# A hybrid SSD, GLA and ConvFFN decoder step: alternating accumulator banks, half a gate projected early, weighted scan steps, a late memory norm and ordered state loads

## The chip, the core and the metric

The kernel runs on one core of a Trainium2 chip. The metric is device microseconds of one execution, lower is better. A core has five engines that run their own instruction streams: TensorE (PE in the profile, with its weight loads as PEld), VectorE (DVE), ScalarE (ACT), GpSimd (POOL) and SyncE (SP). [...] Matmul results land in PSUM, which has eight banks of 512 fp32 words per partition.

## What is computed

One inference step of one layer, for 256 prompt tokens and 8 x 4 sample tokens with the same weights (288 columns in all). All data is fp32.

```python
xn = rmsnorm(x, norm_mix)
z, xbc, dt, q, k, v, r, g_lr, gate_a, gate_b = split(xn @ w_in)
# branch a: causal conv, silu, SSD scan (4 groups of 8 heads), D skip, silu(z), group norm
branch_a = u @ w_ssd_out
# branch b: gated linear attention, 4 heads of 256 keys x 512 values, head norm, silu(r)
branch_b = o @ w_gla_out
merged = sigmoid(gate_a) * branch_a + sigmoid(gate_b) * branch_b
h = x + merged @ w_mix_out
h = h + cross_attend(rmsnorm(h, norm_cross), mem_k, mem_v, w_cq, w_co)   # 256 memory tokens
h = h + conv_ffn(rmsnorm(h, norm_ffn))                                     # w_up, conv of 3, silu gate, w_down
y = rmsnorm(h, norm_final)
```

For the prompt, `mem_k` and `mem_v` are `rmsnorm(mem_prompt, norm_mem) @ w_ck` and `@ w_cv`, and they are outputs too. For the samples they come from a cache. The scans start from zero for the prompt and from `state_ssd` and `state_gla` for the eight samples; the new states are outputs.

## The kernel before

Activations lie transposed: 16 tiles (KT) of 128 features by 288 tokens. Weights stream from HBM, 512 KB at a time, on SP's queue (`wload`, L102 to L105, three buffers `raw`). Each weight tile is split into two parts in a reduced fp32 format: ACT writes `whi` (L97), DVE the remainder `wlo` (L99), five buffers each. `proj_w` (L114) then makes three matmuls of 128 x 128 weights by 288 tokens for each k tile and output tile: high by high (L129), high by low (L130), low by high (L133). Up to two output tiles of a projection are accumulated at a time, in banks from `acc_tile` (L56), one tag with four buffers. Three more banks serve everything else (`mm_tile`), one the long sums of the scans (`la_tile`).

The order of work is written as generators. `proj` (L140) yields once per two k tiles. `weave` (L154) takes the main generator step by step and in between so many steps of a background generator that `n_bg` of them are spread over `n_main` main steps. A scheduler then fixes each engine's order from this program order and its own priorities; `keep_in_program_order` and `high_priority` are hints to it.

- Memory part: `mem_proj` (L287) makes the keys or values of one head, 512 columns, with matmuls L313, L314 and L317. The first runs under a hand-fixed order and prepares its operands on the way (`prep_mem`, L324). At its last k tile it computes the memory norm: a reduction, Ln (L336) and Exp (L337) on ACT; each head is scaled by it when it leaves PSUM. `x_norm` (L370) and `x_prep` (L406) normalise x and build masks (L429, L432) in the background of the next heads.
- Eight units: SSD groups 0 to 3, then GLA heads 0 to 3. In stage n (the loop at L1149) the scan of unit n is the background; the main work is 12 steps of the projections of unit n + 1, the output projection of unit n - 1 (`out_proj`, L890, with the additions L897), and the rest of unit n + 1. `N_MAIN` and `N_BG` are the weave's two counts of each stage. In stage 7 the main work is gate A (`gate_a`, L1111).
- SSD scan (L650): POOL loads decays (`load_decay`, L658), and the sample states in four pairs (`load_state`, L672). States are transposed on TensorE and copied by ACT to `st` (L824), which L807 reads; L834 updates the states, and SP stores them.
- GLA scan (L969): POOL loads eight states of 512 KB (L976), four first, then one more after each of the first four is updated. L1078 multiplies queries by the states of half q = 0 or 1; it reads state 3 or 7 first. L1086 and L1087 update a state, L1090 stores it on SP. States and prompt sums share the buffers of `c4`.
- Gate A: ma, the SSD branch, goes to DRAM (`ma_d`) after stage 4's output projection; `gate_a` reads two tiles at a time, multiplies and stores to `mg_d`. Gate B (L1177) adds both branches. Then come mix_out, cross-attention, and the FFN, whose convolution columns are loaded and transposed (L1425) at its beginning.

Of the kernel before, what the change touches and what calls it, by code (L numbers as in the profile page):

```python
# [8 lines left out]
F32 = mybir.dt.float32  # L9
# [26 lines left out]
N_MAIN = [32, 64, 48, 64, 64, 64, 64, 80]  # L36
N_BG = [48] * 4 + [38] * 4
# [3 lines left out]
def hybrid_step(ctx: ExitStack, tc: tile.TileContext, I: dict, O: list):  # L41
# [14 lines left out]
    def acc_tile():  # L56
        return ps.tile([P, 512], F32, tag="acc", bufs=4, name="acc")
# [140 lines left out]
    def rstd_from(pl, ssq, n, four=False):  # L198
# [13 lines left out]
    bsel = p1.tile([NS, NB, NL], F32, name="bsel")  # L212
    G.affine_select(bsel, ones[0:NS, 0:NS], pattern=[[-4, NB], [0, NL]], compare_op=ALU.is_ge, fill=0.0, base=0,
                    channel_multiplier=1)
    G.affine_select(bsel, bsel, pattern=[[4, NB], [0, NL]], compare_op=ALU.is_ge, fill=0.0, base=3, channel_multiplier=-1)
# [12 lines left out]
    dtbd = p1.tile([P, 32 + 40], F32, name="dtbd")[:, 0:32]  # L228
# [16 lines left out]
    mg_d = dram.tile([P, KT, T], F32, name="mg_d")  # L245
    x_d = dram.tile([P, KT, T], F32, name="x_d")
# [3 lines left out]
    with pool("p0") as p0:  # L250
# [3 lines left out]
        bsel_rep = p0.tile([NS, 4, NS], F32, name="bsel_rep")  # L254
        V.tensor_copy(bsel_rep, bsel.rearrange("p b l -> p (b l)").unsqueeze(1).to_broadcast([NS, 4, NS]))
        bsel_rep = bsel_rep.rearrange("p r t -> p (r t)")
        smask = p0.tile([NS, NS], F32, name="smask")
        G.affine_select(smask, causal[0:NS, 0:NS], pattern=[[-4, NB], [0, NL]], compare_op=ALU.is_ge, fill=0.0, base=0,
                        channel_multiplier=1)
        irep = p0.tile([NS, 4, NS], F32, name="irep")  # L260
        V.tensor_copy(irep, ident[0:NS, 0:NS].unsqueeze(1).to_broadcast([NS, 4, NS]))
# [5 lines left out]
        mrow = p0.tile([KT, P], F32, name="mrow")  # L267
        S.dma_start(out=mrow, in_=I["norm_mem"].rearrange("(t p) -> t p", p=P))
# [8 lines left out]
        def mem_prep(k):  # L277

            a = acc_tile() if k % 2 else mm_tile()
# [3 lines left out]

        mss = p0.tile([P, 2, 4], F32, name="mss")
        mrs = p0.tile([P, 2], F32, name="mrs")

        def mem_proj(w, hd, dst, prep=None):  # L287
# [15 lines left out]
            accs = [acc_tile() for _ in range(2)]  # L303
# [15 lines left out]
            t = p0.tile([P, 2, 512], F32, tag="mp", bufs=2, name="mp")  # L319
            for m in range(2):  # L320
                S.activation(t[:, m, :], accs[m], ACT.Identity, scale=mrs[:, m:m + 1])
            G.dma_start(out=dst[0, :, hd, :].rearrange("(m p) d -> p m d", p=P), in_=t)

        def prep_mem(kk):  # L324
            if kk == 0:
                a = mm_tile()
                TR(a[:, 0:KT], mrow, ident[0:KT, 0:KT])
                V.tensor_copy(gmem, a[:, 0:KT])
# [5 lines left out]
            if kk == KT - 1:  # L334
                V.tensor_reduce(mrs, mss, AX.X, ALU.add)
                S.activation(mrs, mrs, ACT.Ln, scale=1.0 / D, bias=epsc[:, 0:1])  # L336
                S.activation(mrs, mrs, ACT.Exp, scale=-0.5)  # L337

        with tc.manual_schedule(engines={mybir.EngineType.PE, mybir.EngineType.Activation, mybir.EngineType.DVE,
# [4 lines left out]
            run(mem_proj(I["w_ck"], 0, o_pmk, prep_mem))  # L344
# [61 lines left out]
        def x_prep():  # L406
# [21 lines left out]
            a = mm_tile()  # L428
# [682 lines left out]
    def gate_a(t, a):  # L1111
# [9 lines left out]
        if t % 2:  # L1121
            nc.sync.dma_start(out=mg_d[:, t - 1:t + 1, :], in_=m)
# [502 lines left out]
```

## Time and profile before

| What | Value |
|---|---|
| Median of 3 runs | 2608.87 us (2606.83 to 2610.24) |
| The profiled execution's own time | 2607.92 us |
| Its span | 2606.2 us |
| Mean granted TensorE clock | 0.996 |
| Read from and written to HBM | 465.27 MB and 45.48 MB |

In the profile, busy times overlap between engines, and a matmul's length includes its way through the array, so that the distance between two starts, not the length, is what a matmul takes from TensorE. A row of the timeline reads: start, length, engine, line, operation, output and operands, shapes, and how many instructions of one kind follow each other in that row; in brackets stands the idle time of the engine before it and what ended it. Rows of windows give the busy time of each engine and number of instructions in a stretch, the granted clock as a share of full speed, the share of the DMA engines, and GB/s. "DMA to landing" is the time from the issue of a transfer to its completion.

### The profile page before, as it was taken

The numbers are of one execution on the slowest core, as the hardware profiler recorded it, in microseconds if no ns is written. First come the engines' busy times: TensorE is split into PE (matmuls) and PEld (weight loads), VectorE is DVE, ScalarE is ACT, GpSimd is POOL, SyncE is SP. The second block draws the span as 40 slices with busy tenths as digits, with TensorE's granted clock in tenths as the row PEclk, the third lists the DMA queues.
The fourth block names the chain that finished last, engine by engine and source line by source line (L and its number), as shares of the span: only waits on it lengthen the run. The fifth ranks groups of instructions, "written<-read, shape, count | busy, mean of one in ns | idle before, by whom it ended". The sixth has DMA issues, their size and how long they took to land. (4 is left out here: it accounts for less than half of the span.)

```text
span 2606.2 us, 50491 instructions
## 1 busy us (share of the span) xinstructions
PE 2576.2 (99%) x19123; PEld 2473.3 (95%) x19123; DVE 1718.2 (66%) x3683; ACT 1376.2 (53%) x2796; POOL 308.2 (12%) x425
## 2 busy tenths in 40 slices
PE   8999999999999999999999999999999999999998
PEld 7889999999989998999999989899999999999998
DVE  5655786886766566666666555567777677675765
ACT  7655655564645463534455544455545454454545
POOL 2003021100000000000000222202202020110200
PEclk9999999999999999999999999999999999999999
DMA  7666566665676666777666778655555555555553
GB/s 250 208 225 205 179 200 179 201 195 148 201 234 212 199 213 218 225 233 237 182 207 214 246 262 298 213 166 168 166 170 166 168 161 172 168 160 178 164 171 126
DMA packets 435280, 514.07 MB, mean 197 GB/s; under 512 B 23208, under 2 KB 384984, under 8 KB 434716
## 3 DMA queue, kind: packets, MB, share of 16 engines
q1 hardware_dynamic: 408684, 423.16, 52.5%
q0 software_dynamic: 26320, 87.68, 10.1%
q8 instruction: 150, 2.46, 0.4%
q14 instruction: 94, 0.77, 0.1%
q10 hardware_dynamic: 32, 0.01, 0.0%
HBM read 465.27 MB, written 45.48 MB: 196 GB/s over the span
## 5 line engine op out<-in xcount | busy, mean ns | idle before, releaser
L99 DVE TENSOR_TENSOR wlo<-raw,whi 128x512 fp32r<-128x512 f32 (+1 forms) x1464 | 989.5, 689 | 703.3 <-ACT whi L97 689.6
L97 ACT CAST whi<-raw 128x512 fp32r<-128x512 f32 (+1 forms) x1464 | 898.2, 618 | 1043.8 <-PE acc L130 824.1
L129 PE MATMUL acc<-xn,whi 128*128 128x288 f32 (+1 forms) x1936 | 551.0, 300 | 2.8 <-ACT whi L97 2.8
L130 PE MATMUL acc<-xn,whi 128*128 128x288 f32 (+1 forms) x1936 | 542.5, 295 | 0.0
L133 PE MATMUL acc<-xn,wlo 128*128 128x288 f32 (+1 forms) x1936 | 413.0, 295 | 1.4 <-DVE wlo L99 1.4
L129 PE MATMUL acc<-hf,whi 128*128 128x288 f32 x1408 | 396.0, 296 | 0.0
L130 PE MATMUL acc<-hf,whi 128*128 128x288 f32 x1408 | 393.5, 295 | 0.0
L129 PEld LDWEIGHTS acc<-xn,whi 128*128 128x128 f32 (+1 forms) x1936 | 365.0, 189 | 10.2 <-issue 6.7
L130 PEld LDWEIGHTS acc<-xn,whi 128*128 128x128 f32 (+1 forms) x1936 | 365.2, 189 | 4.2 <-issue 1.0
L133 PEld LDWEIGHTS acc<-xn,wlo 128*128 128x128 f32 (+1 forms) x1936 | 311.3, 188 | 1.8 <-DVE wlo L99 1.7
L133 PE MATMUL acc<-hf,wlo 128*128 128x288 f32 x1408 | 302.2, 296 | 0.0
L130 PEld LDWEIGHTS acc<-hf,whi 128*128 128x128 f32 x1408 | 265.1, 188 | 0.1
L129 PEld LDWEIGHTS acc<-hf,whi 128*128 128x128 f32 x1408 | 264.7, 188 | 0.1
L133 PEld LDWEIGHTS acc<-hf,wlo 128*128 128x128 f32 x1408 | 225.4, 188 | 0.0
L130 PE MATMUL acc<-pr,whi 128*128 128x288 f32 x704 | 196.6, 295 | 0.0
L129 PE MATMUL acc<-pr,whi 128*128 128x288 f32 x704 | 195.9, 294 | 0.0
L129 PE MATMUL acc<-un,whi 128*128 128x288 f32 x512 | 153.3, 315 | 2.3 <-DVE mb L897 1.0
L133 PE MATMUL acc<-pr,wlo 128*128 128x288 f32 x704 | 147.8, 291 | 0.0
L1457 POOL COPY fsp<-fst 128x16 f32<-128x16 f32 x88 | 105.4, 1222 | 335.3 <-ACT fcg L1463 87.8
L130 PE MATMUL acc<-un,whi 128*128 128x288 f32 x512 | 143.2, 295 | 0.0
L130 PEld LDWEIGHTS acc<-pr,whi 128*128 128x128 f32 x704 | 132.4, 188 | 0.0
L129 PEld LDWEIGHTS acc<-pr,whi 128*128 128x128 f32 x704 | 132.1, 188 | 0.0
(525 smaller groups left out, 4245.3 us busy)
## 6 DMA issues: line engine op xcount, KB each, us to landing
raw<-in_w_in_dram SPq DMA_DIRECT2D x240, 512.0 KB
raw<-in_w_up_dram SPq DMA_DIRECT2D x176, 512.0 KB
raw<-in_w_down_dram SPq DMA_DIRECT2D x88, 512.0 KB
raw<-in_w_ck_dram SPq DMA_DIRECT2D x32, 512.0 KB
raw<-in_w_cv_dram SPq DMA_DIRECT2D x32, 512.0 KB
raw<-in_w_ssd_out_dram SPq DMA_DIRECT2D x32, 512.0 KB
sin<-in_state_gla_dram POOLq DMA_DIRECT2D x32, 512.0 KB, 5.7
out_dram<-sin SPq DMA_DIRECT2D x32, 512.0 KB
```

The costliest lines, as they stand in the source:

```text
L97: S.copy(hi, raw)
L99: V.tensor_tensor(lo, raw, hi, ALU.subtract)
L129: MM(a, hi[:, k, cs], xh, start=(k0 + s0 + k == 0), stop=False)
L130: MM(a, hi[:, k, cs], xl, start=False, stop=False)
L133: MM(a, lo[:, k, cs], xh, start=False, stop=(k0 + s0 + k == nk - 1))
L1457: G.tensor_copy(sp[:, :, 0:2], st.rearrange("p (b k) -> p b k", k=2))
```

## The change

- Accumulators come from two tags, `acc0` and `acc1`, with two banks each; each projection takes the other tag than the one before it.
- The memory norm's reduction, Ln and Exp and the scaling of the first head move out of the first `mem_proj` into `x_norm`, after four of its steps; the first head stays in its banks until then (`held`). `x_norm` is spread over two heads, `x_prep` over the next two. Masks are made by POOL selections, without the two matmuls of L429 and L432.
- Four of the eight column pairs of gate A are projected in stage 0 (`gate_early`), their tanh kept in DRAM (`ga_d`), and multiplied into ma in the output projection of unit 3 (`branch_a`), which also stores ma on SP four tiles at a time. Stage 7 projects the other four, and its stores go from SP to POOL. `steps` takes 16 steps in place of 12 ahead of the output projection.
- Steps of the scans that handle states count 1.5 (SSD) or 1.25 (GLA) in `weave`.
- `load_decay` reads the 256 prompt columns in place of 288. State loads are kept in program order on POOL.
- L1078's matmuls get high priority in the scheduler.
- The FFN's convolution columns and the final gains are loaded and transposed before gate B's end. `qs` has one buffer in place of two.

```diff
--- before.py
+++ after.py
-N_MAIN = [32, 64, 48, 64, 64, 64, 64, 80]
-N_BG = [48] * 4 + [38] * 4
+N_MAIN = [64, 64, 48, 64, 64, 64, 64, 48]
+N_BG = [58] * 4 + [42] * 4
...
-    def acc_tile():
-        return ps.tile([P, 512], F32, tag="acc", bufs=4, name="acc")
+    turn = [0]
+    def acc_tiles(n):
+        turn[0] += 1
+        return [ps.tile([P, 512], F32, tag=f"acc{turn[0] % 2}", bufs=2, name="acc") for _ in range(n)]
...
     def proj_w(load, ncol, X, nk, cons, N=T):
-        accs = [acc_tile() for _ in range(nt)]
+        accs = acc_tiles(nt)
...
     def weave(main, bg, n_main, n_bg):
-                if next(bg, STOP) is STOP:
+                w = next(bg, STOP)
+                if w is STOP:
                     break
-                done += 1
+                done += 1 if w is None else w
...
+        for r in range(4):
+            q = slice(r * NS, (r + 1) * NS)
+            G.affine_select(smask4[q], causal[q, q], pattern=[[-4, NB], [0, NL]], compare_op=ALU.is_ge, fill=0.0, base=0,
+                            channel_multiplier=1)
+            G.affine_select(bmask[q], ones[q, 0:NB], pattern=[[-4, NB]], compare_op=ALU.is_ge, fill=0.0, base=0,
+                            channel_multiplier=1)
+            G.affine_select(bmask[q], bmask[q], pattern=[[4, NB]], compare_op=ALU.is_ge, fill=0.0, base=3,
+                            channel_multiplier=-1)
+        V.tensor_copy(smaski, smask4)
...
-        mrow = p0.tile([KT, P], F32, name="mrow")
-        S.dma_start(out=mrow, in_=I["norm_mem"].rearrange("(t p) -> t p", p=P))
+        mrow = p0.tile([P, P], F32, name="mrow")
+        V.memset(mrow, 0.0)
+        S.dma_start(out=mrow[0:KT], in_=I["norm_mem"].rearrange("(t p) -> t p", p=P))
...
-        def mem_proj(w, hd, dst, prep=None):
+        def mem_proj(w, hd, dst, prep=None, hold=None):
...
-            accs = [acc_tile() for _ in range(2)]
+            accs = acc_tiles(2)
...
+            if hold is None:
+                rows()
+            else:
+                hold.append(rows)
         def prep_mem(kk):
...
-            if kk == KT - 1:
-                V.tensor_reduce(mrs, mss, AX.X, ALU.add)
-                S.activation(mrs, mrs, ACT.Ln, scale=1.0 / D, bias=epsc[:, 0:1])
-                S.activation(mrs, mrs, ACT.Exp, scale=-0.5)
...
-            run(mem_proj(I["w_ck"], 0, o_pmk, prep_mem))
+            run(mem_proj(I["w_ck"], 0, o_pmk, prep_mem, held))
...
         def x_norm():
+            for _ in range(4):
+                yield
+            V.tensor_reduce(mrs, mss, AX.X, ALU.add)
+            S.activation(mrs, mrs, ACT.Ln, scale=1.0 / D, bias=epsc[:, 0:1])
+            S.activation(mrs, mrs, ACT.Exp, scale=-0.5)
+            yield
+            yield
+            held.pop()()
+            yield
...
-        weave(mem_proj(I["w_cv"], 0, o_pmv), x_norm(), KT, 18)
-        weave(chain(mem_proj(I["w_ck"], 1, o_pmk), mem_proj(I["w_cv"], 1, o_pmv)), x_prep(), 2 * KT - 2, 19)
+        weave(chain(mem_proj(I["w_cv"], 0, o_pmv), mem_proj(I["w_ck"], 1, o_pmk)), x_norm(), 2 * KT, 24)
+        weave(chain(mem_proj(I["w_cv"], 1, o_pmv), mem_proj(I["w_ck"], 2, o_pmk)), x_prep(), 2 * KT - 2, 18)
...
-            G.dma_start(out=ab, in_=acum_d[h0 + 2 * q:h0 + 2 * q + 2, :].partition_broadcast(P))
+            G.dma_start(out=ab[:, :, 0:SEQ], in_=acum_d[h0 + 2 * q:h0 + 2 * q + 2, 0:SEQ].partition_broadcast(P))
...
-                G.dma_start(out=sin[:, e, :].rearrange("p (t n) -> p t n", n=P),
-                            in_=I["state_ssd"][2 * q + e, h0:h0 + 8].rearrange("(t e) x n -> (e x) t n", e=2))
+                tc.keep_in_program_order(G.dma_start(
+                    out=sin[:, e, :].rearrange("p (t n) -> p t n", n=P),
+                    in_=I["state_ssd"][2 * q + e, h0:h0 + 8].rearrange("(t e) x n -> (e x) t n", e=2)))
...
                 sts.append(st)
-                yield
+                yield 1.5
...
-    def out_proj(w, g, u, dst):
+    def out_proj(w, g, u, dst, post=None):
...
+                if post:
+                    post(t)
...
-            G.dma_start(out=sin, in_=I["state_gla"][b, h].rearrange("(k p) v -> p k v", p=P))
+            tc.keep_in_program_order(G.dma_start(out=sin, in_=I["state_gla"][b, h].rearrange("(k p) v -> p k v", p=P)))
...
         for q in range(2):
-            for k in (1, 0):
-                for j in (3, 2, 1, 0):
-                    b = 4 * q + j
-                    MM(osa[NS * j:NS * j + NS, :], qdm[:, k, b, :], sins[b][:, k, :], start=False, stop=(q == 1 and k == 0))
+            with tc.high_priority(2000):
+                for k in (1, 0):
+                    for j in (3, 2, 1, 0):
+                        b = 4 * q + j
+                        MM(osa[NS * j:NS * j + NS, :], qdm[:, k, b, :], sins[b][:, k, :], start=False,
+                           stop=(q == 1 and k == 0))
...
                     V.scalar_tensor_tensor(sin[:, k, :], sin[:, k, :], eb[:, k, SEQ + 4 * b + 3:SEQ + 4 * b + 4], a,
                                            ALU.mult, ALU.add)
-                    yield
+                    yield 1.25
...
-    def gate(o, cons_t):
-        for j2 in range(KT // 2):
+    def gate(o, cons_t, j0=0, j1=KT // 2):
+        for j2 in range(j0, j1):
...
+    gq = []
+    GH = KT // 4
+    def gate_early(t, a):
+        if t % 2 == 0:
+            gq.append(e2("gq"))
+        S.activation(gq[-1][:, t % 2, :], a, ACT.Tanh, scale=0.5)
+        if t % 2:
+            G.dma_start(out=ga_d[:, t - 1:t + 1, :], in_=gq[-1])
+    def gated(m, th):
+        V.scalar_tensor_tensor(m, th, 1.0, m, ALU.add, ALU.mult)
+    def branch_a(t):
+        if t < 2 * GH:
+            if t % 2 == 0:
+                gq.append(e2("gq"))
+                G.dma_start(out=gq[-1], in_=ga_d[:, t:t + 2, :])
+            gated(ma[:, t, :], gq[-1][:, t % 2, :])
+        if t % 4 == 3:
+            nc.sync.dma_start(out=(mg_d if t < 2 * GH else ma_d)[:, t - 3:t + 1, :], in_=ma[:, t - 3:t + 1, :])
...
-            nc.sync.dma_start(out=mg_d[:, t - 1:t + 1, :], in_=m)
+            G.dma_start(out=mg_d[:, t - 1:t + 1, :], in_=m)
...
-        if n == 3:
-            for q in range(4):
-                nc.sync.dma_start(out=ma_d[:, 4 * q:4 * q + 4, :], in_=ma[:, 4 * q:4 * q + 4, :])
...
-        nxt = start(n + 1) if n < 7 else gate(O_GA, gate_a)
+        nxt = start(n + 1) if n < 7 else gate(O_GA, gate_a, GH)
-        parts = [nxt] if n == 0 else [steps(nxt, 12), project(n - 1), nxt]
+        parts = [nxt, gate(O_GA, gate_early, 0, GH)] if n == 0 else [steps(nxt, 16), project(n - 1), nxt]
...
+    def ffn_cols():
+        a = mm_tile()
+        for i in range(4):
+            TR(a[:, i * P:(i + 1) * P], frow[:, i, :], ident)
+        V.tensor_copy(fcol, a.rearrange("p (a t) -> p a t", t=P)[:, :, 0:88])
...
+    late.append(ffn_cols)
     run(gate(O_GB, gate_b))
...
-                qs = px.tile([P, T], F32, tag="qs", bufs=2, name="qs")
+                qs = px.tile([P, T], F32, tag="qs", bufs=1, name="qs")
```

More of the change, by code (lines that the diff above doesn't have):

```diff
@@ L318, in mem_proj, with rows @@
                 yield
[L319 to L322, printed above, removed]
+            def rows():
+                t = p0.tile([P, 2, 512], F32, tag="mp", bufs=2, name="mp")
+                for m in range(2):
+                    S.activation(t[:, m, :], accs[m], ACT.Identity, scale=mrs[:, m:m + 1])
+                G.dma_start(out=dst[0, :, hd, :].rearrange("(m p) d -> p m d", p=P), in_=t)
+            if hold is None:
+                rows()
+            else:
+                hold.append(rows)
         def prep_mem(kk):
@@ L1182, in gate_b @@
         split_from(*mx(t), th, 0.5)
+    fcol = pb.tile([P, 4, 88], F32, name="fcol")
+    gfin = pb.tile([P, KT], F32, name="gfin")
+    frow = pc.tile([P, 5, P], F32, name="frow")
+    G.memset(frow, 0.0)
+    for i in range(5):
+        src = I["ffn_conv_w"][i] if i < 3 else I["ffn_conv_b"] if i == 3 else I["norm_final"]
+        G.dma_start(out=frow[0:88 if i < 4 else KT, i, :], in_=src.rearrange("(t p) -> t p", p=P))
+    def ffn_cols():
[3 more added lines that the diff above has]
+        V.tensor_copy(fcol, a.rearrange("p (a t) -> p a t", t=P)[:, :, 0:88])
+        a = mm_tile()
+        TR(a[:, 0:P], frow[:, 4, :], ident)
+        V.tensor_copy(gfin, a[:, 0:KT])
     hx = []
```

50 lines of the change are left out of this document (11 added, 39 removed).

## The prediction

> **What bounds the kernel now.** I read the page's busy shares first, then TensorE's timeline in a quiet stage, then the view of TensorE's waits, and last the timelines around each wait.
>
> ```profile
> PE 2576.2 (99%) x19123; PEld 2473.3 (95%) x19123; DVE 1718.2 (66%) x3683; ACT 1376.2 (53%) x2796; POOL 308.2 (12%) x425
> ...
> 2000.05 0.29 PE L129 MATMUL acc<-hf,whi 128*128 128x288 f32 x1
> 2000.19 0.29 PE L130 MATMUL acc<-hf,whi 128*128 128x288 f32 x1
> ```
>
> TensorE is busy for 99% of the span. Its rows overlap: each 288-wide matmul has a length of 0.29 us, but the next starts 0.13 to 0.14 us later. So 0.134 us is the price of one, and only time in which TensorE stands still or is clocked down can be won. The view of waits lists where it stands still:
>
> ```profile
> PE acc L313 <- ACT whi L97: 5.2, 2, 3.4
> PE acc L129 <- ACT whi L97: 2.8, 1, 2.8
> PE la L807 <- ACT st L824: 2.0, 1, 2.0
> PE mm L834 <- ACT st L824: 1.7, 1, 1.7
> PE acc L133 <- DVE wlo L99: 1.4, 1, 1.4
> ...
> PE acc L129 <- DVE mb L897: 1.0, 1, 1.0
> PE acc L129 <- DVE ma L897: 0.9, 1, 0.9
> ...
> PE mm L1425 <- DMA frow<-in_ffn_conv_w_dram: 0.6, 1, 0.6
> ```
>
> The columns are us in all, times, longest. These rows sum to 15.6 us, of which 13.8 are the eight long stalls (the first row's other 1.8 us belong to the start). So this is a change worth tenths of a per cent at most, and anything it adds counts.
>
> **Part 1: the memory norm applied late.** The two heaviest stalls carry a half-rate clock behind them. The first is at 32 us:
>
> ```profile
> 31.94 1.28 ACT L336 ACT_TABLE_LOAD   x1
> ...
> 35.56 1.12 ACT L97 CAST whi<-raw 128x512 fp32r<-128x512 f32 x2
> ...
> 36.22 0.53 PE L313 MATMUL acc<-whi,mn_hi 128*128 128x512 f32 x1 [3.41 <-ACT whi L97]
> ...
> 36.30:40.00 3.70, 3.70 (x10) 2.89 (x11) 2.40 (x4) 3.50 (x8) 0.00 (x0) 0.54 0.96 361
> ```
>
> ACT loads its Ln table, computes, loads its Exp table and only then converts weights again (L97); TensorE waits 3.41 us. The last row is a window (length, busy time of PE, PEld, DVE, ACT, POOL, granted clock, DMA share, GB/s): clock 0.54 for 3.7 us, which loses 3.7 x 0.46 = 1.7 us. In the new order on ACT, four conversions stand ahead of the Ln load and further ones between the two loads; one conversion feeds six 512-wide matmuls (two row tiles by three passes), and at 0.23 us from start to start four conversions last for 5.5 us, twice the two loads of 1.28. I leave 0.5 us for what shows. Gain 3.4 + 1.7 - 0.5 = 4.6.
>
> **Part 2: state loads in order, less decay loaded, scan over 64 steps (stage n = 0).**
>
> ```profile
> 238.24 2.14 POOL L658 DMA_DIRECT2D ab<-acum_d  x4
> 240.37 3.71 POOL L672 DMA_DIRECT2D sin<-in_state_ssd_dram  x5
> ...
> 238.94 1.77 SPq L567 DMA_DIRECT2D out_dram<-cst  x2
> 240.82 2.33 SPq L104 DMA_DIRECT2D raw<-in_w_in_dram  x3
> ...
> 251.66 1.14 ACT L97 CAST whi<-raw 128x512 fp32r<-128x512 f32 x2 [9.64 <-DMA raw<-in_w_in_dram]
> ...
> 249.10 0.43 PE L133 MATMUL acc<-xn,wlo 128*128 128x288 f32 x2
> 252.34 0.61 PE L129 MATMUL acc<-xn,whi 128*128 128x288 f32 x1 [2.80 <-ACT whi L97]
> ...
> 251.40:258.40 7.00, 6.06 (x25) 6.07 (x26) 6.06 (x17) 6.05 (x19) 1.79 (x3) 0.51 0.55 171
> ```
>
> POOL issues four decay loads and five state loads back to back while SP stands at two stores; the weights behind them arrive 9.64 us late for ACT, TensorE stands still for 2.80 us, and the clock is 0.51 for 7 us, which loses 7.0 x 0.49 = 3.4. In the changed order POOL's state loads come some 60 us of TensorE work later, behind copies of the scan, and only the four smaller decay loads (256 for 288 KB) stay in this place. Gain 2.8 + 3.4 = 6.2. The st waits of L807 and L834 and the wlo wait (2.0 + 1.7 + 1.4) lie in scans of n = 0 and n = 1. Stage 0 gets 64 main steps in place of 32, so its scan is half as dense, and I count the 2.0 in full; n = 1 keeps 64 steps with weights that spread the heavy ones, and I count two thirds of 3.1, between nothing and all. Gain 2.0 + 2.1 = 4.1.
>
> **Part 3: two bank pairs.** L897 adds a finished accumulator into ma or mb, and the next projection's L129 waits 1.0 and 0.9 us for its bank. In the new program's order at least 4 us of matmuls stand between the last matmul of a bank and its next use, where out_proj had 0.9 before. Gain 1.9. **The FFN columns** loaded early take the 0.6 us of L1425 away. Rows of idle time understate a stall by some 0.17 us: from 249.10 two matmuls of 0.134 end at 249.37, and 249.37 to 252.34 is 2.97, against 2.80 shown. Eight stalls give 1.3 more. Sum of gains: 4.6 + 6.2 + 4.1 + 1.9 + 0.6 + 1.3 = 18.7 us.
>
> **Costed at nothing.** The early half of gate A is the same projection in another stage; its tanh on ACT, eight DMAs of two tiles each way and multiplies on DVE lie under TensorE, since ACT is busy for 53% and DVE for 66%. Without that cover they would cost as the wlo row does, 1.4 us apiece at worst. Stores of mg_d now stand on SP ahead of weights in project(3); a store held back there acts as the cst store did, but with one store per four tiles instead of nine loads beside it. For this and for DVE's denser stages I take 0.5 us, between 0 and one wlo stall of 1.4. Masks without matmuls and SP copies moved are within 0.4 us of work.
>
> **Part 4: the wait that the change adds.** The GLA scan reads eight states, four at a time. The second four matmul groups (L1078, q = 1) begin with state 7, whose buffer is that of state 1: update of state 1 (L1086 and L1087), store on SP (L1090), load on POOL (L976), landing. In the kernel before, this chain is hidden by the four updates between:
>
> ```profile
> 766.60 0.40 PE L1086 MATMUL mm<-vst,kb 128*128 128x512 f32 x1
> 767.81 0.38 SPq L1090 DMA_DIRECT2D out_dram<-sin  x1
> 773.04 0.72 POOL L976 DMA_DIRECT2D sin<-in_state_gla_dram  x1 [7.88 <-DVE sin L1087]
> DMA to landing us min/median/max: 6.4/6.4/6.4
> 780.57 1.92 PE L1078 MATMUL la<-sin,qdm 128*32 128x512 f32 x16
> ...
> 889.56 0.40 PE L1086 MATMUL mm<-vst,kb 128*128 128x512 f32 x1
> L976 POOL DMA_DIRECT2D sin<-in_state_gla_dram x1: 724/724/724, 895.5 to 895.5; - x1
> DMA to landing us min/median/max: 6.2/6.2/6.2
> ...
> 1013.70 0.40 PE L1086 MATMUL mm<-vst,kb 128*128 128x512 f32 x1
> L976 POOL DMA_DIRECT2D sin<-in_state_gla_dram x1: 731/731/731, 1019.0 to 1019.0; - x1
> DMA to landing us min/median/max: 5.3/5.3/5.3
> ...
> 1147.98 0.40 PE L1086 MATMUL mm<-vst,kb 128*128 128x512 f32 x1
> L976 POOL DMA_DIRECT2D sin<-in_state_gla_dram x1: 723/723/723, 1156.9 to 1156.9; - x1
> DMA to landing us min/median/max: 6.7/6.7/6.7
> ```
>
> From the update to the landing that makes 12.8 us at n = 4 (773.04 + 6.4 - 766.60), 12.1 at n = 5, 10.6 at n = 6, and 15.6 at n = 7; L1078 starts 13.97 us after the update at n = 4, so nothing waits. High priority moves these matmuls ahead of updates that stood before them. Counting the new order at 0.134 us per 288-wide and 0.23 us per 512-wide matmul (0.40 less 0.17 of overlap), TensorE has 9.9, 8.1, 8.3 and 8.2 us of work left between update 1 and the q = 1 matmuls. All else on TensorE is queued behind the waiting matmul, so this wait is lost in full. With the shortest chain, 10.6, the four waits are 0.7 + 2.5 + 2.3 + 2.4 = 7.9 us; with the four as measured 2.9 + 4.0 + 2.3 + 7.4 = 16.6; with 15.6 for all 27.9. I take 11.4, between the middle two stages, since weights stop flowing when TensorE stands: 1.5 + 3.3 + 3.1 + 3.2 = 11.1 us. Three of these stand at the edge of the idle time that halved the clock (2.80), and one of 2.0 (L807) did not halve it. I count one episode at 1.7, the lighter of the two seen, between none and three at 3.4.
>
> The Trainium skill, "TensorE: Matmul & The Clock Gate", Part 1, says that the clock halves after an idle window of about 3.4 us in a grid that runs freely. The 3.41 us stall agrees; the 2.80 us one halved the clock too, earlier than the page has it. By the page's figure none of my waits would clock TensorE down and the time would be 1.7 us less; by the 2.80 row all three would, at up to 3.4 each, 8.5 us more.
>
> **Sum.** The profiled execution took 2607.9 us. 2607.9 - 18.7 + 0.5 + 11.1 + 1.7 = 2602.5. That execution is 0.95 us below the median of 2608.87, within its spread, and I leave it so.
>
> **The rivals.**
> (a) No new wait: the chain fits into the 8 to 10 us left. For it: SP issues a store 1.2 us after the update, and with fewer bytes beside it a load may land faster. Against it: none of the four chains was below 10.6. Time 2607.9 - 18.7 + 0.5 + 1 = 2591.
> (b) The other side, slower: the GLA wait with the clock behind it. If the chain stays at 12.8 or more the waits are 2.9 + 4.7 + 4.5 + 7.4 = 19.5 us, and with four half-rate episodes between 1.7 and 3.4 they cost 28. Time 2607.9 - 18.2 + 28 = 2618. It decides once waits and episodes pass 18.2 + 6.2 us. For it: n = 4 and n = 7 measured so; against it: n = 5 and n = 6.
> (c) Pinned loads starve the weights:
>
> ```profile
> q1 hardware_dynamic: 408684, 423.16, 52.5%
> q0 software_dynamic: 26320, 87.68, 10.1%
> ```
>
> Eight state loads of one SSD scan now stand back to back on POOL (2.1 MB). Weights on SP's queue come in packets of 1.04 KB (423.16 MB in 408684), POOL's in 3.3 KB. In n = 1 to 3 conversions lead TensorE by some 10 us in the new order, where the wait at 251.66 was 9.64. If one of them runs dry, it costs what 249 did, 2.8 + 3.4 = 6.2: 2602.5 + 6.2 = 2609, and 2615 with two. The Trainium skill, "DMA: Bandwidth & Descriptors", section on queues, rings and completion order, says that an engine goes round its queues packet by packet; by an estimate from that rule and these sizes POOL would take three quarters of the engines during such a burst. The 9.64 us wait agrees with it.
> (d) The stalls only move: SSD waits come back in other steps, half of the 18.7 lost. Time 2612. For it: 66% DVE with weights on the same engine; against it: the new order gives more distance in each place.
>
> **How the numbers follow.** Forecast 0.42, (a) 0.23, (b) 0.15, (c) 0.10, (d) 0.10. The forecast's own range is 2597 to 2608. About 0.2%, 5.2 us, is what a measurement of this kernel can tell from no change, so faster is below 2603.7 and slower above 2614.1. Faster: all of (a) and 0.27 of the forecast, 0.50. Same: 0.15 of the forecast, 0.06 of (c), 0.07 of (d), 0.28. Slower: (b) and the rest, 0.22. Range 2589 to 2615: it holds (a) and the forecast and ends within (b).
>
> **What would show it.** Right: no wait near 32 and 249 us and full clock there; no row of L129 waiting for ma or mb; rows of the q = 1 matmuls waiting for the state load, about 1.5 us at n = 4 and 3 us at n = 5 to 7. Wrong: no such wait (then (a)); a clock below 0.6 behind each of them (then (b)); ACT's conversions waiting for weights beside a burst of eight state loads (then (c)); new waits for st or wlo in the SSD stages (then (d)).

## The result and the profile after

The changed kernel is slower. Its median is 2626.14 us (2623.59 to 2628.56, 4 runs) against 2608.24 us for the kernel before on the same chip (4 runs), a ratio of 1.0068 with a 95% interval of 1.005 to 1.0085. The profiled execution took 2624.57 us, with a span of 2622.9 us and a mean granted clock of 0.993.

Busy shares on the page after, and the head of TensorE's waits (us in all, times, longest):

```profile
PE 2574.6 (98%) x19119; PEld 2471.1 (94%) x19119; DVE 1718.3 (66%) x3680; ACT 1375.6 (52%) x2796; POOL 315.1 (12%) x443
```

```profile
PE la L1092 <- DMA sin<-in_state_gla_dram: 23.6, 4, 7.8
PE acc L133 <- DVE xsT L592: 3.8, 3, 1.6
PE acc L319 <- ACT whi L101: 3.2, 3, 1.7
PE mm L890 <- DVE sqa L881: 1.7, 1, 1.7
PE mm L845 <- DVE wst L623: 1.4, 1, 1.4
```

TensorE's busy time is 1.6 us shorter than before while its span grew by 16.7 us. The first row is new: the matmuls of the GLA scan (L1092 now, L1078 before) wait four times for a state load, 23.6 us in all. The eight stalls that the prediction listed in the kernel before are gone from the list or smaller; the rows for xsT, sqa and wst, tiles that DVE writes in the SSD stages, are new or grown, and small.

The timeline of the changed kernel around the wait at n = 4 (update of state 1, store, load, first matmul with state 7), on TensorE, SP and POOL:

```profile
799.71 0.40 PE L1101 MATMUL mm<-vst,kb 128*128 128x512 f32 x1
800.40 0.34 SPq L1146 DMA_DIRECT2D ma_d<-ma  x1
801.05 0.38 SPq L1105 DMA_DIRECT2D out_dram<-sin  x1
807.18 0.34 SPq L1146 DMA_DIRECT2D ma_d<-ma  x1
810.01 0.72 POOL L989 DMA_DIRECT2D sin<-in_state_gla_dram  x1 [9.13 <-DVE wlo L103]
817.31 3.64 PE L1092 MATMUL la<-sin,qdm 128*32 128x512 f32 x16 [7.76 <-DMA sin<-in_state_gla_dram]
820.88 0.61 PE L134 MATMUL acc<-xn,whi 128*128 128x288 f32 x1
```

From the update at 799.71 to the matmul at 817.31 it takes 17.6 us. TensorE had run out of other work at 817.31 - 7.76 = 809.55, 9.84 us after the update, where the count of the new order had said 9.9. The 16 matmuls then took 3.64 us, against 1.92 in the kernel before, and the 288-wide one behind them has a length of 0.61 in place of 0.29: that is the half clock. The other three stages, in the same view:

```profile
932.33 0.40 PE L1101 MATMUL mm<-vst,kb 128*128 128x512 f32 x1
933.54 0.38 SPq L1105 DMA_DIRECT2D out_dram<-sin  x1
939.68 0.72 POOL L989 DMA_DIRECT2D sin<-in_state_gla_dram  x1 [6.95 <-DMA out_dram<-sin]
946.84 1.94 PE L1092 MATMUL la<-sin,qdm 128*32 128x512 f32 x8 [6.49 <-DMA sin<-in_state_gla_dram]
...
1063.39 0.40 PE L1101 MATMUL mm<-vst,kb 128*128 128x512 f32 x1
1064.74 0.38 SPq L1105 DMA_DIRECT2D out_dram<-sin  x1
1072.50 0.72 POOL L989 DMA_DIRECT2D sin<-in_state_gla_dram  x1 [8.57 <-DVE kb L1098]
1077.88 1.94 PE L1092 MATMUL la<-sin,qdm 128*32 128x512 f32 x8 [6.20 <-DMA sin<-in_state_gla_dram]
...
1183.10 0.40 PE L1101 MATMUL mm<-vst,kb 128*128 128x512 f32 x1
1184.31 0.38 SPq L1105 DMA_DIRECT2D out_dram<-sin  x1
1188.32 0.72 POOL L989 DMA_DIRECT2D sin<-in_state_gla_dram  x1 [2.25 <-DVE wlo L103]
1194.39 2.49 PE L1092 MATMUL la<-sin,qdm 128*32 128x512 f32 x12 [3.13 <-DMA sin<-in_state_gla_dram]
```

Chains of 14.5, 14.5 and 11.3 us, with 8.0, 8.3 and 8.2 us of work to cover them. Windows behind the four waits (length, busy times and counts of PE, PEld, DVE, ACT, POOL, then granted clock, DMA share, GB/s):

```profile
817.30:826.00 8.70, 8.69 (x47) 5.57 (x48) 2.04 (x3) 2.22 (x4) 0.00 (x0) 0.69 0.00 0
946.80:955.00 8.20, 8.16 (x43) 5.14 (x44) 1.61 (x3) 1.82 (x3) 0.00 (x0) 0.66 0.12 23
1077.90:1086.00 8.10, 8.10 (x47) 5.08 (x48) 2.04 (x3) 2.16 (x4) 0.00 (x0) 0.74 0.18 43
1194.40:1201.00 6.60, 6.60 (x38) 3.82 (x39) 1.94 (x4) 1.83 (x3) 0.00 (x0) 0.74 0.27 94
```

Length times the missing share of the clock gives 2.7 + 2.8 + 2.1 + 1.7 = 9.3 us. Waits and half clock together are 32.9 us; the prediction had 11.1 + 1.7 = 12.8. With the measured numbers in its sum, 2602.5 - 12.8 + 32.9 = 2622.6, it comes within 2 us of the profiled 2624.57; as the account below shows, that closeness is in part luck, since the gains in this sum are not where the prediction had them.

### The profile page after: what moved, and what is told of

Read it like the earlier page. It is cut to its first block, busy times and chain, and to the rows that moved or that the text cites. A ratio compares the mean times of both kernels' runs of the same rounds, so it can differ in the third digit from the quotient of the medians.

```text
span 2622.9 us, 50482 instructions
## 1 busy us (share of the span) xinstructions
PE 2574.6 (98%) x19119; PEld 2471.1 (94%) x19119; DVE 1718.3 (66%) x3680; ACT 1375.6 (52%) x2796; POOL 315.1 (12%) x443
## 5 line engine op out<-in xcount | busy, mean ns | idle before, releaser
L103 DVE TENSOR_TENSOR wlo<-raw,whi 128x512 fp32r<-128x512 f32 x1464 | 989.6, 689 | 711.0 <-ACT whi L101 695.6
L101 ACT CAST whi<-raw 128x512 fp32r<-128x512 f32 x1464 | 896.7, 618 | 1024.5 <-PE acc L134 816.0
L134 PEld LDWEIGHTS acc<-xn,whi 128*128 128x128 f32 (+1 forms) x1936 | 365.4, 189 | 10.6 <-issue 8.3
L133 PE MATMUL acc<-un,whi 128*128 128x288 f32 x512 | 147.5, 304 | 3.8 <-DVE xsT L592 3.8
L134 PE MATMUL acc<-un,whi 128*128 128x288 f32 x512 | 143.4, 296 | 0.5 <-DVE un L171 0.5
```

The source lines that it names most:

```text
L101: S.copy(hi, raw)
L103: V.tensor_tensor(lo, raw, hi, ALU.subtract)
L133: MM(a, hi[:, k, cs], xh, start=(k0 + s0 + k == 0), stop=False)
L134: MM(a, hi[:, k, cs], xl, start=False, stop=False)
```

## The experiments

Where a run is of "the changed kernel without priority", it is the changed kernel with this edit alone:

```diff
         for q in range(2):
-            with tc.high_priority(2000):
-                for k in (1, 0):
+            for k in (1, 0):
...
```

**The priority taken away.** The first run, and the same kernel a second time beside other variants:

> The changed kernel with the high priority of the q = 1 (and q = 0) matmuls of the GLA scan taken away, all else kept. In its order TensorE has 18.7, 18.7, 18.7 and 13.9 us of matmuls between the update of state 1 and the matmul that reads state 7. Theory (the early matmuls wait for the chain store, load, landing, and the half-rate clock follows): the four waits of 23.6 us and their clock episodes of some 10 us go, so 2590 to 2594 us, faster than the kernel before. Rival A (the chain is slow because of the ordered loads or the weighted steps, and shows wherever the matmuls stand): waits of several us stay at this line, 2605 to 2626. Rival B (another part of the change costs the time, and the wait only moves): no wait at this line, but the time stays above 2608.

> The kernel without priority once more, beside its variants on one chip. Earlier ratio to the kernel before 0.9945. Theory: 0.993 to 0.996.

Measured: 2590.57 us (5 runs), ratio 0.9945 (0.9931 to 0.9959), and 2589.23 us (5 runs), 0.9931 (0.9917 to 0.9944). No wait for a state is left on the list. At n = 5, on TensorE, SP and POOL:

```profile
919.83 0.40 PE L1100 MATMUL mm<-vst,kb 128*128 128x512 f32 x1
921.04 0.38 SPq L1104 DMA_DIRECT2D out_dram<-sin  x1
927.39 0.72 POOL L989 DMA_DIRECT2D sin<-in_state_gla_dram  x1 [7.17 <-DMA out_dram<-sin]
938.28 1.92 PE L1091 MATMUL la<-sin,qdm 128*32 128x512 f32 x16
```

Store to load takes 6.35 us, about as long as with the priority (6.14), but the matmul stands 18.45 us behind the update and meets the state long landed, at full clock (1.92 us). Both rivals fall: the waits are gone and so is the loss. Against the kernel before, the kernel without priority is 0.5 to 0.7% faster.

**The priority alone, in the kernel before.**

```diff
         for q in range(2):
-            for k in (1, 0):
+            with tc.high_priority(2000):
+                for k in (1, 0):
...
```

> The kernel before with the high priority alone. Its order leaves 8.0 us of matmuls between the update of state 1 and the matmul that reads state 7, in each of the four GLA stages. Theory: with the chains measured in the kernel before (12.8, 12.1, 10.6, 15.6 us) waits of 4.8, 4.1, 2.6 and 7.6, 19 us in all, and half-rate episodes of 1.7 to 3.4 us behind each, 7 to 14: 2634 to 2641. Rival A (the other parts lengthen the chain, the priority alone is harmless): within 5 us of the kernel before.

Measured: 2635.26 us (4 runs), ratio 1.0111 (1.0095 to 1.0126). The four first matmuls with state 7:

```profile
785.39 1.08 PE L1079 MATMUL la<-sin,qdm 128*32 128x512 f32 x4 [5.56 <-DMA sin<-in_state_gla_dram]
914.17 1.08 PE L1079 MATMUL la<-sin,qdm 128*32 128x512 f32 x4 [3.60 <-DMA sin<-in_state_gla_dram]
1043.15 1.08 PE L1079 MATMUL la<-sin,qdm 128*32 128x512 f32 x4 [3.56 <-DMA sin<-in_state_gla_dram]
1184.02 1.93 PE L1079 MATMUL la<-sin,qdm 128*32 128x512 f32 x8 [5.14 <-DMA sin<-in_state_gla_dram]
```

Waits of 17.9 us, near the 19 expected in all (stage by stage 5.6, 3.6, 3.6 and 5.1 against 4.8, 4.1, 2.6 and 7.6), and 28 us lost; the rest is half clock and other waits that grew beside it (the wait for ma from 0.9 to 2.7 us). The priority does the harm by itself.

**Why the chain grew from 12.1 and 10.6 to 14.5 us at n = 5 and 6.** The GLA scan unweighted and spread as before, priority kept:

```diff
-N_BG = [58] * 4 + [42] * 4
+N_BG = [58] * 4 + [38] * 4
...
-                    yield 1.25
+                    yield
```

> The changed kernel, priority kept, with the GLA scan's steps unweighted and spread as before (38 in place of 42). Its order leaves 8.0, 8.0, 8.0 and 8.2 us of matmuls ahead of the state 7 matmul, so the distance is the same as in the changed kernel. Theory (denser scan steps put more state traffic into the same microseconds and so lengthen store, load and landing from 12.2 and 10.7 to 14.5 and 14.4 us at n = 5 and 6): chains of 11 to 12.5 us there, waits of 3 to 4.5 us in place of 6.5 and 6.1, and 2614 to 2620 us. Rival (the ordered loads lengthen the chain): chains of 14 us stay, and the time stays at 2624 to 2628.

Measured: 2620.46 us (5 runs), ratio 1.004 (1.0025 to 1.0055), just above the 2614 to 2620 expected. At n = 5:

```profile
943.26 0.40 PE L1101 MATMUL mm<-vst,kb 128*128 128x512 f32 x1
944.48 0.38 SPq L1105 DMA_DIRECT2D out_dram<-sin  x1
948.74 0.72 POOL L989 DMA_DIRECT2D sin<-in_state_gla_dram  x1 [6.72 <-DVE wlo L103]
954.34 1.08 PE L1092 MATMUL la<-sin,qdm 128*32 128x512 f32 x4 [2.93 <-DMA sin<-in_state_gla_dram]
```

The chain is 11.1 us here (10.8 at n = 6), with the ordered loads and the priority as they were. So it is the weighted scan that lengthened it: store to load is 4.3 us against 6.1. At n = 4 the chain was still 14.6, and at n = 7 it was 13.0; there three other runs with the priority have 12.8 to 13.1, and the changed kernel's 11.3 is the lowest. "Denser" is true of one place only: at n = 5 the stores of states 0 and 1 go out 5.2 us apart in the changed kernel (928.38 and 933.54) and 6.8 us apart here (937.66 and 944.48), so that POOL's load of state 6, which follows the first store, starts 1.6 us ahead of the second one (931.98) and not 3.2 us (941.26). The next update comes later than here, 8.2 us after state 1's first and not 5.2. That the load beside it is what slows the store is argued from these rows; no run tests it alone.

**The store on another queue.**

```diff
-                nc.sync.dma_start(out=o_sgla[b, h].rearrange("(k p) v -> p k v", p=P), in_=sin)
+                S.dma_start(out=o_sgla[b, h].rearrange("(k p) v -> p k v", p=P), in_=sin)
```

> The changed kernel, priority kept, with the GLA states stored from ACT's queue in place of SP's. Theory of the chain's length (the store stands in SP's queue behind one or two 512 KB weight loads, so its end comes 4 to 9 us after its issue): store to load falls to some 3 us, each wait shrinks by 2 to 5 us, and the time to some 2610. Rival (the transfers share the same 16 engines, and a store takes as long from any queue): store to load stays at 4 to 9 us, time 2620 to 2630.

Measured: 2626.7 us (2 runs), ratio 1.0077 (1.0059 to 1.0096). At n = 4, on ACT's queue and POOL:

```profile
802.59 0.38 ACTq L1105 DMA_DIRECT2D out_dram<-sin  x1
812.18 0.72 POOL L989 DMA_DIRECT2D sin<-in_state_gla_dram  x1 [10.02 <-DMA out_dram<-sin]
```

9.6 us from store to load, against 9.0 from SP's queue; at n = 5 to 7 the chains are 14.7, 15.3 and 12.8 us, none shorter than in the changed kernel. My theory of a place behind weights in SP's queue falls; the rival, shared engines, stands.

**The stores of ma at n = 4.** The first attempt changed nothing and decides nothing: the four stores were written behind the output projection, but two of them were still issued beside the state's store (0.7 us ahead of it in SP's timeline, as in the changed kernel).

```diff
         if t % 4 == 3:
-            nc.sync.dma_start(out=(mg_d if t < 2 * GH else ma_d)[:, t - 3:t + 1, :], in_=ma[:, t - 3:t + 1, :])
...
         yield from out_proj(I["w_ssd_out"] if kind == "s" else I["w_gla_out"], i, fin[n], dst, branch_a if n == 3 else None)
+        if n == 3:
+            for t in range(3, KT, 4):
+                nc.sync.dma_start(out=(mg_d if t < 2 * GH else ma_d)[:, t - 3:t + 1, :], in_=ma[:, t - 3:t + 1, :])
```

> The changed kernel, priority kept, with the four stores of ma (576 KB each) issued together after the output projection, in place of one after each four tiles. Theory (at n = 4 these stores share the DMA engines with the state's store and lengthen the chain to 17.6 us): the n = 4 chain falls to some 14.5 us as at n = 5 and 6, its wait from 7.8 to some 4.7, and the time to some 2622. Rival (the n = 4 chain is long for another reason): it stays at 17 us, and the time at 2625.

Measured: 2624.81 us (4 runs), ratio 1.0067 (1.0051 to 1.0082), a chain of 17.3 us at n = 4. The second attempt issues the same four stores at the beginning of stage 5, kept in program order:

> The changed kernel, priority kept, with the four stores of ma held back to the beginning of stage 5. Before the state 7 matmul of n = 4 its order leaves 8.3 us. Theory (two of these 576 KB stores, issued 0.7 us before the state's store and 6.1 us after it, lengthen the n = 4 chain from some 14.4 to 17.6 us): a chain of 14 to 15 us at n = 4, a wait of some 6 in place of 7.8, and a time some 2 us lower, 2622 to 2625. Rival (n = 4 is long because of DVE or the weights): the chain stays at 17 us.

Measured: 2623.53 us (4 runs), ratio 1.0059 (1.0043 to 1.0074); the difference in time to the changed kernel is within the spread. The timeline at n = 4 shows the chain all the same:

```profile
804.82 0.40 PE L1101 MATMUL mm<-vst,kb 128*128 128x512 f32 x1
806.16 0.38 SPq L1105 DMA_DIRECT2D out_dram<-sin  x1
812.02 0.72 POOL L989 DMA_DIRECT2D sin<-in_state_gla_dram  x1 [6.83 <-DVE ma L908]
```

Store to load is 5.9 us in place of 9.0, the chain 13.7 in place of 17.6; the wait falls only to 5.4 us, since this order leaves 8.3 us and not 9.8. So the stores of ma lengthen the chain at n = 4. The best version below, which holds them back too, repeats it without the priority: 6.4 us from store to load, where the kernel without priority has 9.4. The two causes overlap there: the light scan took 3.0 us off the same chain (17.6 to 14.6), but its steps also moved two stores of ma, to 4.9 us ahead of the state's store and 1.3 us behind it (808.53 and 814.76 around 813.43).

**What the gains are made of**, each with one part undone in the kernel without priority. Gate A whole in stage 7 and 32 main steps in stage 0:

```diff
-N_MAIN = [64, 64, 48, 64, 64, 64, 64, 48]
-N_BG = [58] * 4 + [42] * 4
+N_MAIN = [32, 64, 48, 64, 64, 64, 64, 80]
+N_BG = [58] * 4 + [42] * 3 + [54]
...
-        nxt = start(n + 1) if n < 7 else gate(O_GA, gate_a, GH)
+        nxt = start(n + 1) if n < 7 else gate(O_GA, gate_a)
...
-        parts = [nxt, gate(O_GA, gate_early, 0, GH)] if n == 0 else [steps(nxt, 16), project(n - 1), nxt]
+        parts = [nxt] if n == 0 else [steps(nxt, 16), project(n - 1), nxt]
```

> The kernel without priority, with gate A projected whole in stage 7 as before, so that stage 0 has 32 main steps again and ma goes to DRAM in one form. The state loads stay ordered. If the stall at 249 us and its half clock (6.2 us) went away by the order of the loads, and 345 us's 2.0 us by the longer stage 0, the time is 2 us above the run without priority, 2591 to 2594, with a wait at the st copy again. Rival (the longer stage 0 alone removed both): 6 to 9 us above, 2597 to 2600, and a wait for weights in stage 0. If the early gate gained nothing: within 1 us.

Measured: 2600.58 us (6 runs), ratio 0.9971 (0.9958 to 0.9983), which by the ratios and medians is 7 to 11 us above the kernel without priority. But its list of waits has

```profile
PE acc L133 <- DVE xsT L592: 3.7, 3, 1.8
PE la L1091 <- DMA sin<-in_state_gla_dram: 3.5, 1, 3.5
```

and the second row is a state wait in stage 7, at 1111 us, which this edit's steps brought with them, with a clock of 0.76 for 7.0 us behind it (1.7 us). That leaves 2 to 6 us for the early gate and the longer stage 0. Two more stretches of half clock, 3.4 us each from 388.9 and 470.8 us, take up to 3.4 of these; they stand behind waits for xsT and sqa of which the kernel without priority has shorter ones at full clock. So a gain of the early gate is not shown. No long wait for weights came back in stage 0, only one of 1.3 us for wlo (at 252 us), and of the st wait that was expected 0.7 us came back. The SSD state loads set free to move, in the kernel without priority:

> The kernel without priority, with the SSD state loads free to move on POOL again; five of the eight of stage 0 then go ahead of copies. If the order of the loads is what took the stall of 249 us away (6.2 us by the prediction), a wait of ACT or TensorE for weights comes back in stage 0, and the time is 3 to 7 us above the run without priority. Rival (the longer stage 0 and smaller decay loads alone did it): within 1.5 us, and no such wait.

Measured: 2591.13 us (6 runs), ratio 0.9935 (0.9922 to 0.9949), not to be told apart in time from the kernel without priority beside it (0.9931). In its timeline and a window behind it, however, the stall is back:

```profile
239.73 3.74 POOL L682 DMA_DIRECT2D sin<-in_state_ssd_dram  x5
...
255.98 0.54 PE L137 MATMUL acc<-xn,wlo 128*128 128x288 f32 x2 [2.97 <-DVE wlo L103]
...
258.00:260.00 2.00, 2.00 (x11) 2.00 (x10) 1.20 (x4) 2.00 (x6) 1.73 (x3) 0.50 0.93 270
```

Five loads behind the decay loads again, 2.97 us of standstill and a half clock afterwards. In the kernel without priority, where the loads are ordered, TensorE is busy for all of 195 to 260 us at full clock. So the order does remove that stall. What made up for it stands on the list of waits: the rows for xsT (2.2 us) and wst (1.4) of the kernel without priority beside it are missing here. With the order, the eight loads of a stage go out together, and the xsT waits follow such a burst; an example is given below, at rival (c). So the order won one stall and gave 3.6 us of waits back.

Two further parts: accumulators in one tag, and the memory norm computed at the end of the first head.

> As the run without priority, and accumulators in one tag of four banks as before. If the alternating pairs are worth what the prediction counted, the waits for ma and mb (1.0 and 0.9 us) come back and the time is 2 us above the run without priority. Rival: the pairs themselves make the new bank waits seen in the changed kernel (first matmul of a projection for DVE's xsT and ma, 3.8 us on the wait list), and the time is 2 to 4 us below it. If neither, within 1 us.

> The kernel without priority, with the memory norm computed at the end of the first head as before. Theory of the prediction: it was worth 4.6 us, so 4.6 us above the run without priority, with 3.4 us of wait near 36 us and half clock behind. Rival (in the run without priority waits of 2.2 and 1.6 us at the same kind of conversion stand at 39 and 55 us, so most of the gain was given back): 1 to 2 us above.

Measured: 2588.9 us (5 runs), ratio 0.9932 (0.9919 to 0.9944), and 2592.35 us (5 runs), 0.9936 (0.9922 to 0.9949). Both lie between the two runs of the kernel without either edit (0.9931 and 0.9945), so neither part is worth an amount that can be measured. With the norm at the end of the first head, the stall near 36 us is back (2.34 us, then a clock of 0.55 for 3.7 us). With the late norm, though, a stall of the same matmuls stands some 5 us later: 0.63 us at 40 us in the changed kernel, 2.25 us at 41 us without priority, and 3.34 us at 43 us in the run with one tag, there with a clock of 0.51 for 3.0 us behind it. The conversions that ended the last two had themselves waited for weights, 1.87 and 3.51 us. The L897 waits for ma and mb stay away with one tag too; an ACT ma wait of 0.7 us (L905) is all that shows.

The weights of the scans:

> The kernel without priority, with all steps of the SSD scan counted as one (48 steps). Theory A (weights move the light end of the scan together, which makes the new waits for sqa, xsT and wst of 2.0, 1.8 and 1.4 us): those shrink, st waits of 1.4 to 1.7 us return near 445 us, and the time is within 2 us of the run without priority. Theory B (weights gained what the prediction said, two thirds of 3.1 us): 2 us above it, with the sqa wait still there.

> No priority and no weights in either scan (48 and 38 steps). The order leaves 13.9, 13.9, 13.9 and 12.3 us for the state 7 chain. By the chains of the run with the light GLA scan (14.6, 11.0, 10.7, 12.9) waits of 0.7 and 0.6 us at n = 4 and 7, none between. Time 2585 to 2591, within 2 us of the run with the even SSD scan. Rival (the weights were worth something without the priority): 3 us or more above the run without priority.

Measured: 2587.15 us (4 runs), ratio 0.9914 (0.9901 to 0.9928), and 2592.66 us (5 runs), 0.9941 (0.9929 to 0.9953). Even SSD steps cost nothing: sqa's 2.0 us of L890 and wst's 1.4 disappeared, a bank wait of 2.8 (xsT) and one of 1.5 for the GLA scan's sqa came, and the st waits expected near 445 us did not. With the GLA steps even as well, the distance falls to 13.9 and 12.3 us and three state waits return, 3.6 us in all. Two are at state 7, 0.9 us at n = 4 and 1.6 at n = 7, where the chains were 14.9 and 14.1 us, longer than expected; the third, 1.1 us at n = 7, is at the first four states.

**The best version**, with no priority, even SSD steps, and the stores of ma in stage 5:

> No priority, SSD steps unweighted, stores of ma at the beginning of stage 5. The order leaves 18.7, 18.7, 18.7 and 13.9 us for the state 7 chain; with the stores out of the way of n = 4 its chain of 18.5 us falls to 15, so all four are covered. Theory: 2585 to 2590, ratio 0.991 to 0.994, no wait for the GLA state. Rival (the held stores delay the first work of stage 5): a new wait near the start of stage 5 and 2590 or more.

Measured: 2587.19 us (5 runs), ratio 0.9926 (0.9913 to 0.9938), without any state wait. It beats both kernels, but cannot be told apart from the run with the even SSD scan (0.9914) or from the kernel without priority (0.9931).

## Why the prediction was wrong

**The mechanism was right, its size was not.** Part 4 named the wait, its place, its four occurrences and the distance that the new order leaves (9.9, 8.1, 8.3, 8.2 us; the profile has 9.8, 8.0, 8.3, 8.2). The step that failed is the term "I take 11.4, between the middle two stages, since weights stop flowing when TensorE stands". The chains were 17.6, 14.5, 14.5 and 11.3 us, so the waits were 7.8 + 6.5 + 6.2 + 3.1 = 23.6 and not 11.1. Even without what the change added, the choice was low: with the four chains as measured in the kernel before, the prediction's own sum was 16.6.

- The reason given for choosing low was wrong in its timing. Most of the chain passes while TensorE still works: at n = 4 the store takes from 801.05 to about 810, and TensorE stops at 809.55. Relief that begins with the standstill comes when only the load is left. Nor did it come: in the four standstills the share of the DMA engines was 0.86, 0.76, 0.96 and 1.02, and the four loads took 7.3, 7.1, 5.3 and 6.0 us to landing, against 6.4, 6.2, 5.3 and 6.7 in the kernel before.
- The durations came from the kernel before, but two other parts of the change alter the traffic in that very stretch. The weighted GLA scan made n = 5 and 6 longer by 3.4 and 3.7 us (light scan: 11.1 and 10.8), and the stores of ma made n = 4 longer by 3.9 (17.6 to 13.7 without them). The sum priced each part alone.

**The clock.** One episode of 1.7 us was counted; all four waits were followed by one, 9.3 us in all. This is the second term that was too small. Three of the waits that Part 4 counts (3.1 to 3.3 us) were above the 2.80 us that it took for the edge, so its own row spoke for three; and there is no such edge, as the last section shows: a standstill of 1.9 us halved the clock and one of 3.0 did not.

**The gains.** Predicted 18.7, less 0.5. The kernel without priority is 16.4 and 19.5 us faster than the kernel before in its two groups of runs (2606.94 - 2590.57 and 2608.73 - 2589.23). The sum came out, its parts did not, so its closeness is in part luck. By the pages, idle time (span less PE busy) fell from 30.0 to 23.6 us, and the two stretches of half clock, 5.1 us, went: 11.5 of the 20.9 us by which the two profiled spans differ (2606.2 and 2585.3). The other 9 lie inside TensorE's busy time, and their cause stays open.

- Part 2 held in its place: in the kernel without priority TensorE between 195 and 260 us went from 62.20 us busy at clock 0.95 to 65.00 at 1.00, about 6 us, against 6.2; setting the loads free brought the stall back. In time the order is not seen, since it brought waits of its own.
- Part 1 was too high: ACT's table loads moved, but a stall of L319 that waits for ACT's conversions stayed (3.2 us in all after and 4.7 without priority, where L313 had 5.2), where the conversions now wait for weights themselves (1.87 us without priority), and undoing the part made no difference that can be measured.
- Part 3's waits are gone, but not by the bank pairs, as the run with one tag shows.
- New waits in the SSD stages (xsT, sqa, wst) took some back, as rival (d) has it.

**The rivals.** Rival (a), no new wait, gave 2591, and this is what the kernel without priority takes (2590.57, 2589.23), though not for rival (a)'s reason: its chain is as long, and the matmul merely stands behind it. The changed kernel is that kernel with the wait. Rival (b), the same wait with the clock behind it, gave 2618 from chains "12.8 or more"; it was nearest, and was given 0.15 against 0.42. The rows for it were in the prediction: three of the four chains measured, 12.8, 12.1 and 15.6, were above the value taken. Rival (c) showed its sign, at a small price. In the changed kernel POOL issues eight state loads together at 298, 418 and 543 us; from 544 to 552 us its queue took 77.1% of the DMA engines' time and SP's 15.7%, as the prediction had estimated (three quarters), and ACT then waited 7.22 us for weights, to 556.62. TensorE worked through all of that on weights converted before. But DVE stood behind ACT for 6.82 us, to 557.27, with xsT still to do (L592, at 560.10 us), and TensorE then waited 1.2 and 1.0 us for xsT. That the burst led to these waits is read from the order in time, and agrees with the run with the SSD loads free, where both are gone.

## What to carry to other kernels

When a read is moved ahead, measure the whole chain that must end before it (update, store, completion, reload, landing), and set its longest occurrence, not its middle, against the work left in front of it; a wait at the bottleneck engine is asymmetric, since spare distance costs nothing, while missing distance was paid twice here, as standstill and as half clock. A chain of transfers does not keep its length when another part of the same change moves other transfers beside it, so the parts of a change are to be priced in the stretch where they meet. One small hint to a scheduler can outweigh all the rest: here one line lost 32 to 36 us (ratios 1.0068 less 0.9945 and 0.9931) against 16 to 20 us of gains.

## What the runs showed of the hardware

Moving the state's store from SP's queue to ACT's did not shorten it (9.0 and 9.6 us from store to load at n = 4), with the share of the DMA engines at 0.98 and 0.99 in these stretches: there the engines are the limit and not a place in a queue.

The clock fell after shorter standstills than the 2.80 us of the kernel before: in the light scan's run the wait of n = 6 was 2.63 us, and its 16 matmuls took 3.60 us in place of 1.92. And the fall can come late: with the SSD loads free, work resumed at 255.98 at full clock, and only from about 257.3 did the matmuls' starts stand 0.24 us apart.

```profile
1080.53 3.60 PE L1092 MATMUL la<-sin,qdm 128*32 128x512 f32 x16 [2.63 <-DMA sin<-in_state_gla_dram]
...
257.35 0.44 PE L134 MATMUL acc<-xn,whi 128*128 128x288 f32 x1
257.58 0.44 PE L133 MATMUL acc<-xn,whi 128*128 128x288 f32 x1
```

The first row is from the run with the light GLA scan, the other two from the run with the SSD loads free. In the best version a standstill of 1.92 us (before 559.51) was followed by half clock, and in the run with one tag one of 3.01 us (before 517.72) was not, so the length of the standstill alone does not decide. What fits the traces is the work done in each step of a grid. In each of the 16, all falls lie on one grid of 3.413 us; in the changed kernel they come at 812.46, 945.58, 1075.28 and 1194.75, which are 39, 38 and 35 steps apart. Each stretch of half clock before the end of the kernel lasts one, two or three steps, 3.41, 6.83 or 10.24 us, so the prices of 1.7 and 3.4 us in the prediction are halves of one and two steps. In each of these two runs, a step of the grid and the next one:

```profile
556.09:559.50 3.41, 1.51 (x16) 1.13 (x13) 2.18 (x8) 2.35 (x8) 0.00 (x0) 1.00 0.46 160
559.50:562.92 3.42, 3.41 (x22) 3.14 (x24) 3.42 (x10) 3.30 (x10) 0.00 (x0) 0.50 0.00 0
...
513.14:516.55 3.41, 1.57 (x12) 1.34 (x11) 3.31 (x9) 3.41 (x9) 0.00 (x0) 1.00 0.33 99
516.55:519.97 3.42, 2.25 (x15) 2.17 (x16) 1.63 (x4) 2.36 (x4) 0.00 (x0) 1.00 0.84 252
```

In the best version (first two rows) TensorE was busy for 1.51 us of a step, and the next began at half clock. In the run with one tag the 3.01 us were divided between two steps with 1.57 and 2.25 us of work, and the clock stayed (the share of the clock is the third number from the right). Leaving out the first 20 us and the last 30 us, the traces have 46 falls, each behind a step with at most 1.63 us of work; no step at full clock with more was followed by one, and of those between 1.50 and 1.63 us some were and some were not. This was read from the traces afterwards, and no run was made to test it.

The Trainium skill, "TensorE: Matmul & The Clock Gate", Part 1, puts the fall behind an idle window of about 3.4 us, in a grid of windows that runs freely. The late fall and the grid agree with it; in the length of the standstill the measurement differs, since a step with up to 1.6 us of work in it was enough here.
